# 20 of 22 gate/up pairs of a feed-forward input layer by seven half-size products (Strassen's scheme)

## The chip, the cores and the metric

The kernel runs on one core of one Trainium2 chip. The metric is the device time of one execution in microseconds; the median of three executions of the kernel before is 1820.36 us. Engines are named as in the profile: PE (TensorE matmul), PEld (TensorE weight load), DVE (VectorE), ACT (ScalarE), POOL (GpSimd), SP (SyncE, which issues most DMAs).

## The reference, cut to what matters

The model is two blocks on 512 tokens of width 1024, all in float32. The change is in the feed-forward part of the first block, with D_FF = 2816 = 22 x 128:

```python
hn = rms_norm(h, g_ffn_pre[i])
f_gate, f_up = jnp.split(hn @ w_ffn_in[i], 2, axis=-1)
f = (jax.nn.silu(f_gate) * f_up) @ w_ffn_out[i]
h = h + rms_norm(f, g_ffn_post[i])

h = h + jax.nn.sigmoid(h @ w_ple_gate[i]) * (p[i] @ w_ple[i])
```

where `rms_norm(x, g)` divides each token by the root of its mean square (plus EPS = 1e-6) and multiplies by g.

## The kernel before, in words

Activations are kept transposed: a tile is 128 features by 512 tokens. A linear layer makes one 128-feature output block after another; for each it runs over the 128-feature blocks k of its input, with the weight block as the stationary operand and the tokens as the 512 moving columns, and adds up in one bank of PSUM. Every operand of a product is split into a high part (a rounded copy, made by ScalarE) and a low part (the remainder, made by VectorE), and `mm3` multiplies high by high, high by low and low by high, so that each k-block costs three matmuls.

`prep` loads one weight chunk (128 x 1024, that is eight k-blocks of one output block) into `raw` (two buffers) by a DMA on SP's queue and splits it into `whi` and `wlo` (four buffers each). `step` records work, with or without a weight chunk, in a list; `emit` walks the list and prepares chunks up to two steps ahead of use. That is the order in the source. The order in which instructions stand on each engine is set afterwards by the framework's planner, so an engine's queue can differ from the order of the source. `auxps("mm")` (`mmps`) has five PSUM banks and `auxps("aux")` three. `tmp` is a set of four scratch tiles, `sgt` one of three.

Around the change the work runs thus. `w_out` closes the branch part; its last four output blocks are done by `linear_halves`, first for tokens 0 to 255, then for 256 to 511 with the weights held, and after each half `to_ffn` normalises, adds to `h`, makes the split input `S["B"]` of the feed-forward layer (not yet divided by the root mean square) and that divisor's inverse as a row, `S["R"]`. Then come eight small products (`ple`), written out to DRAM for later. The input layer `w_ffn_in` takes its 44 output blocks in the order gate 0, up 0, gate 1, up 1, ...; pair 0 goes by `linear_halves`, the rest by `linear`, 512 columns wide. `f_in` takes a finished block out of PSUM: a gate block is multiplied by R, passed through SiLU and multiplied by R again; an up block is multiplied by that and split at once into the pair `S["f"][j]`, which the output layer `w_ffn_out` reads. That layer has 22 input blocks, in chunks of 8, 8 and 6, and its last two output blocks are again done in halves. `to_ple` then normalises the result with `rstd_tm` and `rowcast` (small matmuls that sum squares over features and spread the result, and a chain of short VectorE steps), adds to `h`, and feeds `w_ple_gate`, which reloads the eight `ple` tiles.

The helpers hold most line numbers of the profile: L113 is a ScalarE copy (`acopy`), L116 a VectorE operation of two tensors (`tt`), L125 one with a scalar too (`stt`), L168 to L170 are the three matmuls of `mm3`, L205 and L216 the small matmuls of `rstd_tm` and `rowcast`, L697 the SiLU.

Of the kernel before, what the change touches and what calls it, by code (L numbers as in the profile page):

```python
# [15 lines left out]
P = 128  # L16
# [27 lines left out]
def build(tc, d, out):  # L44
# [17 lines left out]
    def fill(pool, taken):  # L62

        n = -taken % LINE
        if n:
            pool.tile([P, n // 4], F32, name="fill")

    fill(tiny, 46 * 32)

# [15 lines left out]
    def blk(pool, tag, bufs, dt=F32, shape=(P, T)):  # L85
        return pool.tile(list(shape), dt, tag=tag, bufs=bufs, name=tag)

    def tmp():
        return blk(small, "t", 4)
# [57 lines left out]
            return self.tiles[i][:, c.start - i * T:c.stop - i * T]  # L147

    def prep(src, hold=None):
        n = src.shape[-1]  # L150
        raw = wp.tile([P, D], F32, tag="raw", bufs=2, name="raw")
        nc.sync.dma_start(raw[:, :n], src)
        if hold is not None:
            hi, lo = [], []
            for c0 in range(0, n, T):
                h, l = hold(), hold()
                m = min(n - c0, T)
                split(raw[:, c0:c0 + m], h[:, :m], l[:, :m])
# [8 lines left out]
    def mm3(ps, wh, wl, xh, xl, first, last):
        pe.matmul(ps, wh, xh, start=first, stop=False)  # L168
        pe.matmul(ps, wh, xl, start=False, stop=False)  # L169
        pe.matmul(ps, wl, xh, start=False, stop=last)  # L170

    def bcast_mid(ap2, n):
        return ap2.unsqueeze(1).to_broadcast([ap2.shape[0], n, ap2.shape[1]])
# [22 lines left out]
        stt(out, t, 5.0, y, ALU.add, ALU.mult)  # L196
        return out

    def rstd_tm(sqs, scale, c=ALL, out=None, tag=""):

        b0, b1 = c.start // P, c.stop // P
        ps = auxps()
        for b in range(b0, b1):
            for i, s in enumerate(sqs):
                pe.matmul(ps[:, b - b0:b - b0 + 1], s[:, (b - b0) * P:(b - b0 + 1) * P], ones[:, 0:1],  # L205
                          start=(i == 0), stop=(i == len(sqs) - 1))
        m = tiny.tile([P, b1 - b0], F32, tag="rs_m" + tag, bufs=2, name="rs_m")
        ts(m, ps[:, :b1 - b0], scale, EPS, ALU.mult, ALU.add)
        return rsqrt_small(m, [P, b1 - b0], out, tag)

    def rowcast(y):

# [76 lines left out]

                step(fn, d[name][n][:, k0 * P:k1 * P], bg)  # L290

    def linear_halves(name, nbs, kb, xs, consume, then=None, hold=None):

        held = {}
        for hf, c in enumerate(HALVES):
            order = [(n, k) for n in nbs for k in kchunks(kb)]
            if hf:
                order.sort(key=lambda nk: nk[1])
            for n, (k0, k1) in order:
                def body(n=n, k0=k0, k1=k1, c=c):  # L300
# [303 lines left out]
    def load_h():  # L604
        st1.close()
        S["hp"] = hp.enter_context(tc.tile_pool(name="hp", bufs=1, reuse_waits="tile"))
        S["pf"] = st2.enter_context(tc.tile_pool(name="pf", bufs=1, reuse_waits="tile"))
        for n in range(NB):
            S["h"][n] = blk(S["hp"], "h", 8)
            nc.scalar.dma_start(S["h"][n], d["xT"][n])  # L610
        S["p"] = []
        for k in range(2):
            t = tmp()
            nc.scalar.dma_start(t, d["pT"][k])
            hi, lo = blk(S["pf"], "fh", 14, F32R), blk(S["pf"], "fh", 14, F32R)
# [13 lines left out]
            S["ss"].add(ps, c)  # L629
        return fn  # L630

    w_out_post = post("g_mix_post", lambda: blk(S["pf"], "fh", 14))

    def to_ffn(c):

        r = rowcast(rstd_tm(S["ss"].parts(c), 1.0 / D, c))
        if c.start == 0:
            S["B"] = [pair("B") for _ in range(NB)]
            S["R"] = blk(small, "R", 1)
            S["ss2"] = SqSum(lambda c: blk(S["pf"], "sx", 2, shape=(P, T // 2)))  # L640
# [13 lines left out]
        acopy(S["R"][:, c], rowcast(rstd_tm(S["ss2"].parts(c), 1.0 / D, c)))  # L654
# [5 lines left out]
    linear_halves("w_out", range(4, NB), 8, xa, w_out_post, to_ffn,  # L660
                  hold=lambda n, k0: (lambda: blk(S["pf"], "fl", 14, F32R)) if n >= 5 else None)

    S["pd"] = [None] * NB

# [21 lines left out]
        return pair(set_)  # L686


    def f_in(n, ps, c):
        R = S["R"][:, c]  # L690
        j = n % NF
        if n < NF:
            if j not in S["sigs"]:
                S["sigs"][j] = sgt()
            t = S["sigs"][j][:, c]
            tt(t, ps, R, ALU.mult)
            act.activation(out=t, in_=t, func=AF.Silu)  # L697
# [12 lines left out]
    ffn_post = post("g_ffn_post", lambda: blk(acts, "th", 8))  # L710


    S["xd"] = [None] * NB

    def to_ple(c):
        r = rowcast(rstd_tm(S["ss"].parts(c), 1.0 / D, c))
# [10 lines left out]
        return (lambda: blk(acts, "tl", 8, F32R)) if n == NB - 1 and k0 < 16 else None  # L727

    linear("w_ffn_out", range(NB - 2), NF, lambda k: S["f"][k], ffn_post)
    linear_halves("w_ffn_out", [NB - 2, NB - 1], NF, lambda k: S["f"][k], ffn_post, to_ple, hold_ffn)  # L730

    def ple_gate(n, ps, c):
        if n == 0 and c.start == 0:
            S["B"] = [None] * NB
            S["pw"] = {}
            S["ss"] = SqSum()
            S["ss"].acc = blk(small, "sq", 3)
        if n not in S["pw"]:
            S["pw"][n] = blk(S["pf"], "fh", 14)
# [649 lines left out]
```

## Time and profile before

| | |
|---|---|
| median of 3 executions | 1820.36 us (1819.8 to 1820.97) |
| profiled execution | 1820.43 us, of which its span 1818.7 us |
| granted TensorE clock | 0.997 |
| busy in the span | PE 1802.5, PEld 1485.9, DVE 1171.5, ACT 743.3 us |
| bytes moved | 189.57 MB, 104 GB/s |
| loads of `w_ffn_in` | 44 of 512 KB, 3.4 us each to landing |

The span runs from the first to the last instruction. Busy time counts an engine's instructions; a matmul overlaps its neighbours, so PE's busy time tells that it had work and not that it ran at its peak. In rows in order of time the first number is the start, the second the length, both in us, and brackets hold the idle time before it and what ended that. `mm<-th,whi` is a matmul that writes a tile `mm` and reads `th` and `whi`; `th` and `tl` hold the high and low parts of the input layer's activations, `fh`, `fl`, `xh`, `xl` those of f. On this time axis pair 0 begins at about 571 us, pair 1 at 583, and the output layer at about 812.

### The profile page before, as it was taken

How to read it: one execution, taken by the hardware profiler on the slowest of the kernel's cores; microseconds unless marked ns; L12 is line 12 of the kernel's file. 1: busy time of each engine (PE TensorE's matmuls, PEld its weight loads, DVE VectorE, ACT ScalarE, POOL GpSimd, SP SyncE). 2: the span in 40 equal slices, each digit the busy share in tenths (PEclk: the TensorE clock that was granted, in tenths of full speed). 3: DMA queues.
4: the chain of work that ended last, by engine and by line, in shares of the span. 5: the costliest groups of instructions: out<-in, count | busy, mean ns of one | idle time of the engine just before them, and what ended most of it. 6: DMA issues, size and time to landing. Idle time of an engine off the chain costs nothing.

```text
span 1818.7 us, 23549 instructions
## 1 busy us (share of the span) xinstructions
PE 1802.5 (99%) x9252; PEld 1485.9 (82%) x9252; DVE 1171.5 (64%) x2062; ACT 743.3 (41%) x1219; POOL 0.7 (0%) x5
## 2 busy tenths in 40 slices
PE   9999999999999999999999999999999999999997
PEld 7888888888888888888898777876678888888887
DVE  6999977996448544442367684587646577777333
ACT  5342234326346323222245762574435354444221
POOL 0000000000000000000000000000000000000000
PEclk9999999999999999999999999999999999999999
DMA  5332323332353232233335222222236322323331
GB/s 193 105 105 94 103 68 107 114 98 67 122 179 100 98 104 93 95 96 96 110 103 189 71 65 77 81 83 82 99 122 204 115 93 93 104 93 92 94 97 65
DMA packets 62895, 189.57 MB, mean 104 GB/s; under 512 B 7232, under 2 KB 10432, under 8 KB 62784
## 3 DMA queue, kind: packets, MB, share of 16 engines
q1 hardware_dynamic: 56736, 177.53, 30.2%
q10 hardware_dynamic: 6048, 10.53, 1.8%
q8 instruction: 72, 1.18, 0.3%
q14 instruction: 39, 0.32, 0.1%
HBM read 176.51 MB, written 11.53 MB: 103 GB/s over the span
## 4 chain that ended last, share of the span: by engine, by line
PE 96%; DVE 2%; ACT 1%; issue 0%; DMA 0%; SPq 0%; DVEq 0%; ACTq 0%
PE mm L169 28%; PE mm L168 28%; PE mm L170 27%; PE g L983 1%; PE att L1111 1%; PE att L170 1%; PE att L169 1%; PE att L168 1%; PE mm L340 1%; PE mm L339 1%; PE mm L341 1%; PE att L1103 1%; PE aux L216 1%; DVE wlo L116 0%; PE att L1082 0%
## 5 line engine op out<-in xcount | busy, mean ns | idle before, releaser
L113 ACT ACTIVATE whi<-raw 128x1024 fp32r<-128x1024 f32 (+3 forms) x304 | 312.3, 1027 | 658.1 <-PE mm L169 405.5
L116 DVE TENSOR_TENSOR wlo<-raw,whi 128x1024 fp32r<-128x1024 f32 (+3 forms) x304 | 359.3, 1182 | 201.2 <-ACT whi L113 198.8
L168 PE MATMUL mm<-xh,whi 128*128 128x512 f32 (+1 forms) x1032 | 393.7, 382 | 0.0
L169 PE MATMUL mm<-xl,whi 128*128 128x512 f32 (+1 forms) x1032 | 393.2, 381 | 0.0
L170 PE MATMUL mm<-xh,wlo 128*128 128x512 f32 (+1 forms) x1032 | 393.1, 381 | 0.0
L169 PE MATMUL mm<-tl,whi 128*128 128x512 f32 (+1 forms) x976 | 379.9, 389 | 0.1
L168 PE MATMUL mm<-th,whi 128*128 128x512 f32 (+1 forms) x976 | 380.0, 389 | 0.0
L170 PE MATMUL mm<-th,wlo 128*128 128x512 f32 (+1 forms) x976 | 378.1, 387 | 0.0
L170 PEld LDWEIGHTS mm<-xh,wlo 128*128 128x128 f32 x1032 | 194.0, 188 | 37.3
L168 PEld LDWEIGHTS mm<-xh,whi 128*128 128x128 f32 x1032 | 193.9, 188 | 37.0 <-issue 0.2
L169 PEld LDWEIGHTS mm<-xl,whi 128*128 128x128 f32 x1032 | 194.0, 188 | 36.7 <-issue 0.2
L168 PEld LDWEIGHTS mm<-th,whi 128*128 128x128 f32 x976 | 183.5, 188 | 38.8 <-issue 4.3
L169 PEld LDWEIGHTS mm<-tl,whi 128*128 128x128 f32 x976 | 183.7, 188 | 36.6 <-issue 2.1
L170 PEld LDWEIGHTS mm<-th,wlo 128*128 128x128 f32 x976 | 183.6, 188 | 35.6 <-issue 1.0
L125 DVE SCALAR_TENSOR_TENSOR cv<-hc,vec,cv 128x507 f32<-128x507 f32 (+18 forms) x240 | 173.0, 736 | 4.2 <-ACT cv L462 0.6
L170 PE MATMUL mm<-fh,wlo 128*128 128x512 f32 (+1 forms) x252 | 91.0, 361 | 0.0
L168 PE MATMUL mm<-fh,whi 128*128 128x512 f32 (+1 forms) x252 | 90.8, 360 | 0.0
L116 DVE TENSOR_TENSOR sg<-mm,R 128x512 f32<-128x512 f32 (+1 forms) x43 | 29.1, 678 | 95.8 <-PE mm L170 95.7
L169 PE MATMUL mm<-fl,whi 128*128 128x512 f32 (+1 forms) x236 | 84.6, 358 | 0.0
L116 DVE TENSOR_TENSOR t<-mm,R 128x512 f32<-128x512 f32 x56 | 38.5, 688 | 54.0 <-PE mm L170 52.0
L116 DVE TENSOR_TENSOR t<-mm,sg 128x512 f32<-128x512 f32 (+1 forms) x31 | 20.9, 674 | 62.5 <-PE mm L170 62.5
L170 PEld LDWEIGHTS mm<-fh,wlo 128*128 128x128 f32 x252 | 47.6, 189 | 7.1
(385 smaller groups left out, 1998.7 us busy)
## 6 DMA issues: line engine op xcount, KB each, us to landing
raw<-in_w_ffn_in SPq DMA_DIRECT2D x44, 512.0 KB, 3.4
raw<-in_w_up SPq DMA_DIRECT2D x44, 512.0 KB, 3.4
raw<-in_w_g SPq DMA_DIRECT2D x24, 512.0 KB, 3.4
raw<-in_w_out SPq DMA_DIRECT2D x16, 512.0 KB, 3.5
raw<-in_w_ffn_out SPq DMA_DIRECT2D x16, 512.0 KB, 3.5
raw<-in_w_gab SPq DMA_DIRECT2D x16, 512.0 KB, 3.4
raw<-in_w_down SPq DMA_DIRECT2D x16, 512.0 KB, 3.6
raw<-in_w_qkv SPq DMA_DIRECT2D x12, 512.0 KB, 3.6
```

The costliest lines, as they stand in the source:

```text
L113: act.activation(out=o, in_=i, func=AF.Copy, scale=scale)
L116: dve.tensor_tensor(out=o, in0=a, in1=b, op=op)
L125: dve.scalar_tensor_tensor(out=o, in0=a, scalar=s, in1=b, op0=op0, op1=op1)
L168: pe.matmul(ps, wh, xh, start=first, stop=False)
L169: pe.matmul(ps, wh, xl, start=False, stop=False)
L170: pe.matmul(ps, wl, xh, start=False, stop=last)
L216: pe.matmul(r[:, b * P:(b + 1) * P], y[:, b:b + 1].to_broadcast([P, P]), ident, start=True, stop=True)
L339: pe.matmul(ps, xh[:, t], wh[:, c], start=(k == 0), stop=False)
L340: pe.matmul(ps, xh[:, t], wl[:, c], start=False, stop=False)
L341: pe.matmul(ps, xl[:, t], wh[:, c], start=False, stop=(k == kb - 1))
L983: pe.matmul(c3(out)[e, b], w(e, b), c3(m)[e, b], start=True, stop=True)
L1103: pe.transpose(pt[:, c:c + P], z[:, c:c + P], ident)
```

## The change

Pairs 0 and 1 stay as they are. For each of pairs 2 to 21 the weights are seen as a 2 x 2 array of blocks a11, a12 (gate, input blocks 0 to 3 and 4 to 7) and a21, a22 (up, the same), and the input as b11, b12 (input blocks 0 to 3, tokens 0 to 255 and 256 to 511) and b21, b22 (blocks 4 to 7). Eight block products become seven, each over four k-blocks, 256 tokens wide and still by `mm3`; the combined weights are formed for every pair on VectorE, the combined activations once (`wino_x`). Products 1, 6, 7, 4 add up in one bank, 5 and 3 in another, 2 has one of its own; partial results are copied or added out between them. A pair's weight groups are {1, 2}, {6, 5}, {7, 3} and {4}; product 4 is done after product 1 of the next pair.

f is written raw by the pairs and split for all 22 blocks in one step (`f_split`) ahead of the output layer. The factor R on f is left out, and the norm behind the output layer makes up for it (`rstd_tm` with `by`, from the kept `S["Rf"]`). The output layer's second half goes through its chunks and k-blocks in reverse. Several buffers have other tags.

```diff
-    def rstd_tm(sqs, scale, c=ALL, out=None, tag=""):
+    def rstd_tm(sqs, scale, c=ALL, out=None, tag="", by=None):
...
+        stt(m, ps[:, :b1 - b0], scale, by, ALU.mult, ALU.mult)
+        tt(m, m, by, ALU.mult)
+        ts(m, m, EPS, None, ALU.add)
+        y = rsqrt_small(m, [P, b1 - b0], out, tag)
+        tt(y, y, by, ALU.mult)
+        return y
...
+    def f_raw(j):
+        S["f"][j] = (blk(S["pf"], "fr", 6) if j < 6 else blk(acts, "xh", 8) if j < 14
+                     else blk(acts, "xl", 8) if j < 21 else tmp())
...
             tt(t, ps, S["R"][:, c], ALU.mult)
             act.activation(out=t, in_=t, func=AF.Silu)
-            tt(t, t, R, ALU.mult)
         else:
-            t = tmp()[:, c]
-            tt(t, ps, S["sigs"][j][:, c], ALU.mult)
-            ...
-            split(t, hi[:, c], lo[:, c])
+            tt(S["f"][j][:, c], ps, S["sigs"][j][:, c], ALU.mult)
...
+    def wino_x(k):
+        x = []
+        for i in (k, 4 + k):
+            x.append(tmp())
+            acopy(x[-1], S["h"][i], v("g_ffn_pre", i))
+        b1, b2 = x
+        r12, r34 = tmp(), tmp()
+        tt(r12[:, H0], b1[:, H1], b1[:, H0], ALU.subtract)
+        tt(r12[:, H1], b2[:, H1], r12[:, H0], ALU.subtract)
+        tt(r34[:, H0], b2[:, H1], b1[:, H1], ALU.subtract)
+        tt(r34[:, H1], b2[:, H0], r12[:, H1], ALU.subtract)
+        for i, r in ((1, r12), (3, r34)):
+            hi, lo = blk(S["pf"], "tc", 16, F32R), blk(S["pf"], "tc", 16, F32R)
+            split(r, hi, lo)
...
+    XOP = {1: 11, 2: 21, 3: 22, 4: 4, 5: 1, 6: 2, 7: 3}
+    FEW = {0: (1, 2), 1: (6, 5), 2: (7, 3), 3: (4,)}
...
+    def weights(p, g):
+        if g == 0:
+            r0 = wp.tile([P, D], F32, tag="raw", bufs=2, name="raw")
+            r1 = blk(S["pf"], "wr", 2, F32, (P, D))
+            nc.sync.dma_start(r0, d["w_ffn_in"][p])
+            nc.sync.dma_start(r1, d["w_ffn_in"][NF + p])
...
+        if g == 1:
+            src = w["c"] = blk(S["pf"], "ws", 1, F32, (P, D))
+            tt(a11, a11, a21, ALU.subtract)
+            tt(src[:, L], a22, a11, ALU.subtract)
+            tt(src[:, R], a21, a22, ALU.add)
+        elif g == 2:
+            tt(a12, a12, w["c"][:, L], ALU.subtract)
+        elif g == 3:
+            src = a22
...
+        split(src, hi[:, :n], lo[:, :n])
+        return hi, lo
...
+    def product(p, m, wh, wl):
+        w = ws.setdefault(p, {})
+        if m in (1, 5, 2):
+            w[m] = (auxps() if m == 2 else mmps())[:, H0]
+        y = w[{1: 1, 6: 1, 7: 1, 4: 1, 5: 5, 3: 5, 2: 2}[m]]
+        for k in range(4):
+            b = slice(k * P, (k + 1) * P)
+            xh, xl = ET[XOP[m], k]
+            mm3(y, wh[:, b], wl[:, b], xh, xl, k == 0 and m in (1, 5, 2), k == 3, skip_group_check=True)
+        if m == 1:
+            w["t"], w["v"], w["sg"] = tmp(), tmp(), sgt()
+            acopy(w["t"][:, H0], y)
+        elif m == 2:
+            tt(w["sg"][:, H0], y, w["t"][:, H0], ALU.add)
+        elif m == 6:
+            acopy(w["t"][:, H1], y)
+        elif m == 5:
+            acopy(w["v"][:, H0], y)
+        elif m == 7:
+            w["f"] = f_raw(p)
+            tt(w["f"][:, H1], y, w["v"][:, H0], ALU.add)
+        elif m == 3:
+            sg = w["sg"]
+            tt(sg[:, H1], y, w["t"][:, H1], ALU.add)
+            tt(sg, sg, S["R"], ALU.mult)
+            act.activation(out=sg, in_=sg, func=AF.Silu)
+            tt(w["f"][:, H1], w["f"][:, H1], sg[:, H1], ALU.mult)
+        else:
+            tt(w["f"][:, H0], y, w["sg"][:, H0], ALU.mult)
 
     order = [n for j in range(NF) for n in (j, NF + j)]
     linear_halves("w_ffn_in", order[:2], 8, xb, f_in)
-    linear("w_ffn_in", order[2:], 8, xb, f_in)
+    for k in range(2):
+        step(lambda k=k: wino_x(k))
+    linear("w_ffn_in", order[2:3], 8, xb, f_in)
+    for k in range(2, 4):
+        step(lambda k=k: wino_x(k))
+    linear("w_ffn_in", order[3:4], 8, xb, f_in)
...
+        if due is None:
+            products(p, 0, (1, 2))
+        else:
+            products(p, 0, (1,))
+            products(due, 3, (4,), [(p, 0, 2)])
+        products(p, 1, (6, 5))
+        products(p, 2, (7, 3))
+        due = p
+    if due is not None:
+        products(due, 3, (4,))
+
+    def f_split():
...
+        for j in range(NF):
+            raw = S["f"][j]
+            S["f"][j] = hi, lo = new(j), new(j)
+            split(raw, hi, lo)
+
+    step(f_split)
...
-        r = rowcast(rstd_tm(S["ss"].parts(c), 1.0 / D, c))
+        r = rowcast(rstd_tm(S["ss"].parts(c), 1.0 / D, c, by=S["Rf"][:, c.start // P:c.stop // P]))
...
-    linear_halves("w_ffn_out", [NB - 2, NB - 1], NF, lambda k: S["f"][k], ffn_post, to_ple, hold_ffn)
+    linear_halves("w_ffn_out", [NB - 2, NB - 1], NF, lambda k: S["f"][k], ffn_post, to_ple, hold_ffn, back=True)
```

The combined activations go to 16 tiles of a buffer set `tc`; `f_split` writes blocks 0 to 7 into these same tiles, 8 to 10 into the raw weight buffers `wr` and `ws`, and the rest into `fr`, `xh` and `xl`, which held raw f.

More of the change, by code (lines that the diff above doesn't have):

```diff
@@ L66, in fill @@
             pool.tile([P, n // 4], F32, name="fill")
-    fill(tiny, 46 * 32)
+    fill(tiny, 47 * 32)
     def lined(n):
@@ L149, in prep @@
     def prep(src, hold=None):
+        if callable(src):
+            return src()
         n = src.shape[-1]
@@ L165, in prep, with mm3 @@
         return hi, lo
[L167 to L170, printed above, removed]
+    def mm3(ps, wh, wl, xh, xl, first, last, **kw):
+        pe.matmul(ps, wh, xh, start=first, stop=False, **kw)
+        pe.matmul(ps, wh, xl, start=False, stop=False, **kw)
+        pe.matmul(ps, wl, xh, start=False, stop=last, **kw)
     def bcast_mid(ap2, n):
@@ L207, in rstd_tm @@
         m = tiny.tile([P, b1 - b0], F32, tag="rs_m" + tag, bufs=2, name="rs_m")
-        ts(m, ps[:, :b1 - b0], scale, EPS, ALU.mult, ALU.add)
-        return rsqrt_small(m, [P, b1 - b0], out, tag)
+        if by is None:
+            ts(m, ps[:, :b1 - b0], scale, EPS, ALU.mult, ALU.add)
+            return rsqrt_small(m, [P, b1 - b0], out, tag)
+        stt(m, ps[:, :b1 - b0], scale, by, ALU.mult, ALU.mult)
[4 more added lines that the diff above has]
+        return y
     def rowcast(y):
@@ L290, in linear, with linear_halves @@
                 step(fn, d[name][n][:, k0 * P:k1 * P], bg)
-    def linear_halves(name, nbs, kb, xs, consume, then=None, hold=None):
+    def linear_halves(name, nbs, kb, xs, consume, then=None, hold=None, back=False):
         held = {}
@@ L297, in linear_halves, with body @@
             if hf:
-                order.sort(key=lambda nk: nk[1])
+                order.sort(key=lambda nk: nk[1], reverse=back)
             for n, (k0, k1) in order:
-                def body(n=n, k0=k0, k1=k1, c=c):
-                    if k0 == 0:
+                ks = list(range(k0, k1))
+                first, last = 0, kb - 1
+                if hf and back:
+                    ks.reverse()
+                    first, last = last, first
+                def body(n=n, k0=k0, ks=ks, first=first, last=last, c=c):
+                    if first in ks:
                         held[n, "ps"] = mmps()
@@ L304, in body @@
                     wh, wl = held[n, k0]
-                    for k in range(k0, k1):
+                    for k in ks:
                         xh, xl = xs(k)
                         w = slice((k - k0) * P, (k - k0 + 1) * P)
-                        mm3(ps, wh[:, w], wl[:, w], xh[:, c], xl[:, c], k == 0, k == kb - 1)
-                    if k1 == kb:
+                        mm3(ps, wh[:, w], wl[:, w], xh[:, c], xl[:, c], k == first, k == last)
+                    if last in ks:
                         consume(n, ps, c)
@@ L614, in load_h @@
             nc.scalar.dma_start(t, d["pT"][k])
-            hi, lo = blk(S["pf"], "fh", 14, F32R), blk(S["pf"], "fh", 14, F32R)
+            hi, lo = blk(S["pf"], "fr", 6, F32R), blk(S["pf"], "fr", 6, F32R)
             split(t, hi, lo)
@@ L630, in post @@
         return fn
-    w_out_post = post("g_mix_post", lambda: blk(S["pf"], "fh", 14))
+    w_out_post = post("g_mix_post", lambda: blk(S["pf"], "tc", 16))
     def to_ffn(c):
@@ L653, in to_ffn @@
                 S["ss2"].add(h, c)
-        acopy(S["R"][:, c], rowcast(rstd_tm(S["ss2"].parts(c), 1.0 / D, c)))
+        if c.start == 0:
+            S["Rf"] = tiny.tile([P, NT], F32, tag="Rf", bufs=1, name="Rf")
+        r = S["Rf"][:, c.start // P:c.stop // P]
+        rstd_tm(S["ss2"].parts(c), 1.0 / D, c, out=r)
+        acopy(S["R"][:, c], rowcast(r))
         if c.start:
@@ L659, in build, with two, new, hold_out @@
     linear("w_out", range(4), 8, xa, w_out_post)
-    linear_halves("w_out", range(4, NB), 8, xa, w_out_post, to_ffn,
-                  hold=lambda n, k0: (lambda: blk(S["pf"], "fl", 14, F32R)) if n >= 5 else None)
+    def two(tag, bufs):
+        kept = []
+        def new():
+            if not kept:
+                t = blk(S["pf"], tag, bufs, F32R, (P, D))
+                kept.extend((t[:, :T], t[:, T:]))
+            return kept.pop(0)
+        return new
+    def hold_out(n, k0):
+        if n < 5:
+            return None
+        return two("wr", 2) if n == 7 else (lambda: blk(S["pf"], "tc", 16, F32R))
+    linear_halves("w_out", range(4, NB), 8, xa, w_out_post, to_ffn, hold=hold_out)
     S["pd"] = [None] * NB
@@ L686, in f_pair @@
         return pair(set_)
+    def f_raw(j):
+        S["f"][j] = (blk(S["pf"], "fr", 6) if j < 6 else blk(acts, "xh", 8) if j < 14
+                     else blk(acts, "xl", 8) if j < 21 else tmp())
+        return S["f"][j]
     def f_in(n, ps, c):
[L690 removed]
         j = n % NF
@@ L695, in f_in @@
             t = S["sigs"][j][:, c]
-            tt(t, ps, R, ALU.mult)
+            tt(t, ps, S["R"][:, c], ALU.mult)
             act.activation(out=t, in_=t, func=AF.Silu)
-            tt(t, t, R, ALU.mult)
         else:
-            t = tmp()[:, c]
-            tt(t, ps, S["sigs"][j][:, c], ALU.mult)
             if S["f"][j] is None:
-                S["f"][j] = f_pair(j, "A")
-            hi, lo = S["f"][j]
-            split(t, hi[:, c], lo[:, c])
+                f_raw(j)
+            tt(S["f"][j][:, c], ps, S["sigs"][j][:, c], ALU.mult)
@@ new lines, in build @@
+    H0, H1 = HALVES
+    ET = {}
+    def wino_x(k):
[12 more added lines that the diff above has]
+            split(r, hi, lo)
+            for e, c in enumerate(HALVES):
+                ET[i + e, k] = hi[:, c], lo[:, c]
+        for i, (n, c) in ((11, (k, H0)), (21, (4 + k, H0)), (22, (4 + k, H1))):
+            ET[i, k] = tuple(t[:, c] for t in xb(n))
@@ new lines, in build @@
+    XOP = {1: 11, 2: 21, 3: 22, 4: 4, 5: 1, 6: 2, 7: 3}
+    L, R = slice(0, T), slice(T, D)
+    FEW = {0: (1, 2), 1: (6, 5), 2: (7, 3), 3: (4,)}
+    wr = {}
+    def weights(p, g):
[4 more added lines that the diff above has]
+            nc.sync.dma_start(r1, d["w_ffn_in"][NF + p])
+            wr[p] = dict(a=r0, b=r1)
+        w = wr[p]
+        a11, a12, a21, a22 = (w[x][:, c] for x in "ab" for c in (L, R))
+        src = w["a"]
+        if g == 1:
[7 more added lines that the diff above has]
+            src = a22
+        n = src.shape[-1]
+        hi = wp.tile([P, D], F32R, tag="whi", bufs=4, name="whi")
+        lo = wp.tile([P, D], F32R, tag="wlo", bufs=4, name="wlo")
+        split(src, hi[:, :n], lo[:, :n])
+        return hi, lo
@@ new lines, in build @@
+    ws = {}
+    def product(p, m, wh, wl):
[27 more added lines that the diff above has]
+            tt(w["f"][:, H0], y, w["sg"][:, H0], ALU.mult)
@@ L707, in build, with products, fn @@
     order = [n for j in range(NF) for n in (j, NF + j)]
     linear_halves("w_ffn_in", order[:2], 8, xb, f_in)
-    linear("w_ffn_in", order[2:], 8, xb, f_in)
+    for k in range(2):
[4 more added lines that the diff above has]
+    linear("w_ffn_in", order[3:4], 8, xb, f_in)
+    kept = {}
+    def products(p, g, ms, after=()):
+        def fn(wh, wl):
+            kept[p, g] = wh, wl
+            for q, g2, m in [(p, g, m) for m in ms] + list(after):
+                c = (L, R)[FEW[g2].index(m)]
+                wh, wl = kept[q, g2]
+                product(q, m, wh[:, c], wl[:, c])
+        step(fn, lambda: weights(p, g))
@@ new lines, in build @@
+    PLAIN = ()
+    due = None
+    for p in range(2, NF):
+        if p in PLAIN:
+            linear("w_ffn_in", [p], 8, xb, f_in)
+            if due is not None:
+                products(due, 3, (4,))
+            due = None
+            linear("w_ffn_in", [NF + p], 8, xb, f_in)
+            continue
+        if due is None:
[6 more added lines that the diff above has]
+        due = p
@@ new lines, in build, with new @@
+    if due is not None:
+        products(due, 3, (4,))
+    def f_split():
+        wide, wide2 = two("wr", 2), two("ws", 1)
+        def new(j):
+            if 8 <= j < 10:
+                return wide()
+            if j == 10:
+                return wide2()
+            if j < 14:
+                return blk(S["pf"], *(("tc", 16) if j < 8 else ("fr", 6)), F32R)
+            return blk(acts, "xh" if j < 18 else "xl", 8, F32R)
+        for j in range(NF):
+            raw = S["f"][j]
+            S["f"][j] = hi, lo = new(j), new(j)
+            split(raw, hi, lo)
@@ L738, in ple_gate @@
         if n not in S["pw"]:
-            S["pw"][n] = blk(S["pf"], "fh", 14)
+            S["pw"][n] = blk(S["pf"], "tc", 16)
             nc.sync.dma_start(S["pw"][n], S["pd"][n])
```

## The prediction

> **What bounds the kernel now.** I read the page first, then busy time by stretch, then single instructions in order of time, then the waits.
>
> ```profile
> span 1818.7 us, 23549 instructions
> ...
> PE 1802.5 (99%) x9252; PEld 1485.9 (82%) x9252; DVE 1171.5 (64%) x2062; ACT 743.3 (41%) x1219; POOL 0.7 (0%) x5
> ...
> DVE  6999977996448544442367684587646577777333
> ...
> PEclk9999999999999999999999999999999999999999
> ...
> PE 96%; DVE 2%; ACT 1%; issue 0%; DMA 0%; SPq 0%; DVEq 0%; ACTq 0%
> ```
>
> TensorE is busy and the chain that ended last runs 96% through it, at full clock. A change gains here only by giving TensorE less to stream, and loses wherever another engine then keeps it waiting. Columns of the next view: the stretch, its length, then busy time and count of PE, PEld, DVE, ACT.
>
> ```profile
> 60.00:180.00 120.00, 120.00 (x564) 100.52 (x563) 118.22 (x177) 43.26 (x52) 0.00 (x0) 1.00 0.29 97
> 594.00:812.00 218.00, 218.00 (x964) 180.56 (x963) 100.52 (x120) 63.12 (x80) 0.00 (x0) 1.00 0.30 96
> 571.50:594.00 22.50, 22.50 (x150) 20.57 (x149) 21.34 (x56) 14.28 (x28) 0.00 (x0) 1.00 0.34 112
> ```
>
> The 20 pairs of the change are the second row: 218 us of nothing but 512-column matmuls, VectorE at 46%. The first row shows that VectorE at 98.5% need not hold TensorE up. The third, the way into the pairs, is already 95% VectorE.
>
> **Price of a half-width matmul.** The change trades 512-column matmuls for more of 256 columns. Pair 0 already runs in halves, so the trace has both. In order of time (start, length):
>
> ```profile
> 571.57 0.28 PE L168 MATMUL mm<-th,whi 128*128 128x256 f32 x1
> ...
> 582.97 0.28 PE L170 MATMUL mm<-th,wlo 128*128 128x256 f32 x1
> 583.09 0.40 PE L168 MATMUL mm<-th,whi 128*128 128x512 f32 x1
> ...
> 573.01 0.19 PEld L169 LDWEIGHTS mm<-tl,whi 128*128 128x128 f32 x1
> 573.13 0.19 PEld L170 LDWEIGHTS mm<-th,wlo 128*128 128x128 f32 x1
> ```
>
> From 571.57 to 583.09 lie pair 0's 96 half-width matmuls (two outputs, two halves, 8 k-blocks, 3 passes): 11.52/96 = 0.120 us each. In the 218 us row there are 964 at full width, about two of them cut at the edges: 218/962 = 0.2266. Half width costs 53% of full width, not half. A pair before is 2 outputs x 8 k-blocks x 3 passes = 48 x 0.2266 = 10.88 us; after, 7 products x 4 k-blocks x 3 passes = 84 x 0.120 = 10.08. Gain 0.80 us a pair, 16.0 in 20.
>
> The Trainium skill, "TensorE: Matmul & The Clock Gate", Back-to-back issue gap, gives 518 cycles for 512 columns and 262 for 256; at its 2.4 GHz 48 x 215.8 ns less 84 x 109.2 ns would be 1.19 us a pair, 23.7 in all (an estimate from that page). The rows decide against it: a fixed 13 ns stands on each matmul here. The same page, in Part 3, says that a weight load overlaps running matmuls only for another row group; that would count against 84 loads instead of 48, but the loads above start 0.12 us apart though each lasts 0.19, so by that rule too the trace disagrees.
>
> **Price of the added VectorE and ScalarE work.** What counts is start to start when an engine is packed:
>
> ```profile
> 439.91 4.27 DVE L116 TENSOR_TENSOR cv<-cv,aux 128x512 f32<-128x512 f32 x7
> ...
> 554.12 0.42 DVE L116 TENSOR_TENSOR h<-h,fh 128x256 f32<-128x256 f32 x1
> 554.45 0.48 DVE L125 SCALAR_TENSOR_TENSOR tl<-h,vec,th 128x256 fp32r<-128x256 f32 x1
> ...
> 600.65 0.69 DVE L116 TENSOR_TENSOR sg<-mm,R 128x512 f32<-128x512 f32 x1 [2.75 <-PE mm L170]
> 601.51 1.23 DVE L116 TENSOR_TENSOR wlo<-raw,whi 128x1024 fp32r<-128x1024 f32 x1 [0.18 <-ACT whi L113]
> 602.66 0.68 DVE L116 TENSOR_TENSOR sg<-sg,R 128x512 f32<-128x512 f32 x1
> ...
> 600.42 1.06 ACT L113 ACTIVATE whi<-raw 128x1024 fp32r<-128x1024 f32 x1 [3.86 <-PE mm L169]
> 601.39 0.62 ACT L697 ACTIVATE sg<-sg 128x512 f32<-128x512 f32 x1
> ...
> 445.69 4.27 ACT L113 ACTIVATE th<-cv 128x512 fp32r<-128x512 f32 x8
> ...
> 542.27 0.47 ACT L113 ACTIVATE fh<-mm,vec 128x256 f32<-128x256 f32 x1 [0.76 <-PE mm L170]
> 542.64 0.38 ACT L227 ACTIVATE sq<-mm 128x256 f32<-128x256 f32 x1
> ```
>
> VectorE: 512 columns (4.27 - 0.69)/6 = 0.60, 256 columns 0.33, 1024 columns 1.14 (601.51 to 602.66, rounded down as the follower was ready). ScalarE: 0.97 for 1024, 0.53 for 512, 0.37 for 256 from PSUM. Three rows also show that queues are not in source order: the low part of a later weight block stands between the two halves of one eviction, so a planner fills idle engine time.
>
> Per pair, VectorE after: four half-block weight sums 4 x 0.60 = 2.40; low parts of three full and one half block 3 x 1.14 + 0.60 = 4.02; evictions of products 2, 7, 3, 4 and the final gate product 5 x 0.33, scaling by R 0.60: 2.25. Sum 8.67, under TensorE's 10.08 by 1.41 us (before: 2 x 1.14 + 4 x 0.60 = 4.68 of 10.88). ScalarE: 3 x 0.97 + 0.53 + 3 x 0.37 + 0.53 = 5.1. TensorE stays the bound of a pair if the planner spends VectorE's slack well. Weight buffers give room: product 1's block is free again after product 2 and due two steps later, 5.8 us, for a ScalarE copy and a subtraction of 2.3.
>
> The tight place is ScalarE's copy of product 6 (then of 5): product 7 (then 3) accumulates into the same bank, one product (12 x 0.12 = 1.44 us) later. Copy 0.38 plus the 0.28 tail of the last matmul fit with 0.8 left, but not behind a 1024-column copy begun just before (0.97). Bounds: 0 to 0.2 us each, 0 to 8 us over 40 copies. I take 0.8, near the low end, because the planner's timing has been near the chip's: the view of waits gives
>
> ```profile
> PE aux L216 <- DVE rs_y L125: 2.9, 5, 2.2
> ```
>
> that is, of the small matmuls it places behind VectorE's chains, one waited 2.2 us and the other four 0.7 together.
>
> **The way in.** Sums of the activations (four blocks of input, each 4 half-width VectorE steps, two 512-column splits, two scaled copies) must precede product 6 of pair 2. VectorE: 4 x (4 x 0.33 + 2 x 0.60) = 10.1 us, plus three weight sums 1.8. VectorE is packed from here on:
>
> ```profile
> 571.54 0.75 DVE L116 TENSOR_TENSOR fh<-fh,aux 128x256 f32<-128x256 f32 x2 [0.87 <-PE aux L216]
> ...
> 593.55 0.42 DVE L116 TENSOR_TENSOR xl<-t,xh 128x256 fp32r<-128x256 f32 x1
> 595.21 0.69 DVE L116 TENSOR_TENSOR t<-mm,sg 128x512 f32<-128x512 f32 x1 [1.24 <-PE mm L170]
> ...
> 586.46 0.34 PE aux L205 x4
> 590.09 0.53 PE aux L216 x4
> ```
>
> It runs out of work at 594.0. Taken out before that: three scalings by R (2 x 0.33 + 0.60), two splits of f (0.66), and one weight block not yet due (1.14): 3.1. So product 6 is ready at 594.0 - 3.1 + 10.1 + 1.8 = 602.8. TensorE would be there at 583.09 + 48 x 0.2266 + 0.87 for the row sums among them (the last two rows) + 24 x 0.120 = 597.7. Stall 5.1; bounds 0 (the planner defers evictions and square sums) to 10 (the chain of copies, sums, copy, subtraction through four scratch buffers runs with holes). I take 5.
>
> **The way out.** f is no longer split pair by pair but in one step of 22 splits ahead of the output layer: VectorE 22 x 0.60 = 13.2, ScalarE 22 x 0.53 = 11.7.
>
> ```profile
> 808.07 0.96 DVE L116 TENSOR_TENSOR wlo<-raw,whi 128x768 fp32r<-128x768 f32 x1
> ...
> 812.61 0.39 PE L168 MATMUL mm<-xh,whi 128*128 128x512 f32 x1
> ```
>
> TensorE consumes an f block every 3 x 0.2266 = 0.68 us, slower than 0.60, so it can follow; but the third weight block of the first output, which before was ready 4 us ahead of that layer (808.07 against 812.61), now stands behind the splits and is due after 16 x 0.68 = 10.9 us. Splits 13.2, last eviction 0.33 and this block 0.9 make 14.4: 3.5 us late without a head start, none if VectorE, which has no next pair to prepare in the last 10 us, does six splits early. Only the destinations free up late (four of them 4.3 us before the end). I take 1.5, bounds 0 to 4.
>
> **Small parts.** Leaving R out of f makes the norm behind the output layer three small VectorE steps longer,
>
> ```profile
> 940.35 0.16 DVE L116 TENSOR_TENSOR rs_t<-rs_m,rs_y 128x2 f32<-128x2 f32 x1
> 940.54 0.16 DVE L125 SCALAR_TENSOR_TENSOR rs_t<-rs_t,rs_y 128x2 f32<-128x2 f32 x1
> ```
>
> 0.2 us each, 0.6 in a chain that feeds the next layer closely: 0.5 (bounds 0 and 1.2, both halves). Weight bytes and SP's issues are the same two 512 KB blocks a pair; SP issues both at a pair's first step, waits at most for the buffer of two pairs earlier, and nothing due sooner queues behind. The reversed order of the output layer's second half frees the first f buffers last, and these take the eight reloads on SP that were issued at 929.0 to 933.5 before; they now start at about 932 and are needed from 941: nothing, up to 2 us if late. Other renamed buffers: nothing, since each is free when asked for.
>
> **Sum**, against the profiled execution's 1820.43 us (0.07 over the median of 1820.36): -16.0 + 0.8 + 5 + 1.5 + 0.5 = -8.2, so 1812.
>
> **Rivals.**
> *In and out hidden.* The planner starts activation sums and splits early enough. For it: ScalarE is 63% busy in the stretch before 594; against it: VectorE's 95%. Time 1820.4 - 16.0 + 1 = 1805.
>
> *Transitions dearer.* The way in costs 10 and the way out 4, or the copies 8: 1818 to 1822, no difference.
>
> *VectorE's queue binds every pair (slower).* Two of the four weight blocks are summed on VectorE, copied on ScalarE (1.06) and subtracted on VectorE. If the order leaves VectorE idle across both copies, a pair is 8.67 + 2 x 1.15 = 11.0 us, longer than 10.88: 1820.4 + 2 + 7.8 = 1830. It decides from about 1.8 us of uncovered idling a pair (8.67 + 1.8 = 10.47: 0.41 gained x 20 = 8.2, all spent on the ends). For it: a pair now passes eleven times between ScalarE and VectorE, the old one six times (weight block twice, gate twice, split twice). Against it: the first stretch above, VectorE 98.5% busy and TensorE unbroken, though its filler work depended on no matmul. The Trainium skill, "VectorE: DVE Perf Modes", The DRAIN you can't avoid, has the next VectorE step start only once the pipe is empty. That would make lengths, not starts, add up; the rows here overlap by 0.08 us (601.51 + 1.23 against 602.66).
>
> **Chances.** Forecast (1808 to 1817) 0.46; hidden 0.12; dearer 0.18; slower (1824 to 1838) 0.24. Two runs of this kernel are told apart from about 0.2%, 3.6 us: faster 0.46 + 0.11 = 0.57, same 0.19, slower 0.24. The range 1804 to 1831 takes in the first three and half of the last; the likeliest case's own is 1808 to 1817.
>
> **What would show it.** Right: 84 half-width matmuls a pair, 0.120 apart, a pair every 10.1 us; VectorE about 86% in the pairs; one TensorE gap near 597 to 603 waiting for VectorE; a smaller one 11 us into the output layer, behind a weight block. Wrong: a pair over 10.4 us with TensorE waiting for weight blocks or for ScalarE's copies; half-width spacing above 0.125; no gap at 597.

## The result, and the profile after

Median of the changed kernel 1809.13 us (1808.77 to 1812.59, four runs), of the kernel before in the same set 1820.08 (1819.25 to 1820.97); ratio 0.9942, interval 0.9929 to 0.9954. So 0.58% faster, 2.9 us under the forecast of 1812. The profiled execution took 1808.77 us (span 1807.0) against 1820.43 (1818.7).

The page of the kernel after:

```profile
span 1807.0 us, 25347 instructions
PE 1787.1 (99%) x9972; PEld 1506.2 (83%) x9972; DVE 1271.6 (70%) x2268; ACT 807.4 (45%) x1334; POOL 0.7 (0%) x5
...
DVE  6999977996448999992286784586546577777333
...
PE 92%; DVE 4%; ACT 2%; DMA 1%; issue 1%; SPq 0%; DVEq 0%; ACTq 0%
```

TensorE has 720 more matmuls and 15 us less to do; 20 x (84 - 48) = 720, so the whole difference in count is the change. VectorE's digits for the slices of the pairs, 5 and 4 before, are 9. The chain of waits still runs through TensorE, but 4% of it is now VectorE. Busy time by stretch of the kernel after (length; busy time and count of PE, PEld, DVE, ACT, POOL; clock, DMA share, GB/s):

```profile
594.00:604.00 10.00, 6.92 (x53) 6.28 (x53) 10.00 (x21) 7.85 (x16) 0.00 (x0) 1.00 0.00 1
604.00:799.40 195.40, 195.40 (x1630) 195.40 (x1630) 180.38 (x280) 110.48 (x167) 0.00 (x0) 1.00 0.34 105
799.40:811.40 12.00, 11.26 (x47) 7.92 (x46) 11.66 (x19) 7.45 (x13) 0.00 (x0) 1.00 0.28 86
```

Way in, pairs, way out. In the first row VectorE is busy for all of 10 us while TensorE lacks three. In the second TensorE never pauses: 195.4/1630 = 0.120 us a matmul, with VectorE at 92%. One pair, from the first matmul of one of its products to the same one of the next pair, in order of time:

```profile
610.78 0.28 PE L170 MATMUL mm<-tc,whi 128*128 128x256 f32 x1
...
620.86 0.28 PE L170 MATMUL mm<-tc,whi 128*128 128x256 f32 x1
```

10.08 us, as forecast. The way in, TensorE (the bracket gives the idle time before, and what ended it):

```profile
597.49 0.28 PE L170 MATMUL mm<-tc,whi 128*128 128x256 f32 x1
598.12 0.38 PE L171 MATMUL mm<-tc,whi 128*128 128x256 f32 x1 [0.35 <-DVE tc L116]
598.35 0.28 PE L172 MATMUL mm<-tc,wlo 128*128 128x256 f32 x1
600.47 0.38 PE L170 MATMUL mm<-tc,whi 128*128 128x256 f32 x1 [1.84 <-ACT t L113]
...
602.33 0.28 PE L172 MATMUL mm<-tc,wlo 128*128 128x256 f32 x1
603.49 0.39 PE L170 MATMUL mm<-th,whi 128*128 128x256 f32 x1 [0.88 <-ACT whi L113]
```

Start to start beyond 0.120 us: 0.51 before 598.12, 2.00 before 600.47, 1.04 before 603.49, and smaller ones; 4.0 together. The largest is put down to ScalarE's copy of a product; ScalarE's and VectorE's own rows say who was late:

```profile
600.03 0.38 ACT L113 ACTIVATE t<-mm 128x256 f32<-128x256 f32 x1 [1.29 <-DVE t L116]
```

```profile
599.18 1.09 DVE L116 TENSOR_TENSOR t<-t 128x256 f32<-128x256 f32 x3
```

ScalarE, next in its queue, stood 1.29 us idle for a VectorE step on a scratch buffer, one of the three sums of activations in the second row. The last of the three gaps is put down to a copy of weights that stood behind this one in ScalarE's queue. The way out, TensorE and then VectorE:

```profile
803.58 0.45 PE L170 MATMUL mm<-tc,whi 128*128 128x512 f32 x1
804.30 0.50 PE L171 MATMUL mm<-tc,whi 128*128 128x512 f32 x1 [0.28 <-DVE tc L116]
...
804.88 0.40 PE L170 MATMUL mm<-tc,whi 128*128 128x512 f32 x1
805.50 0.50 PE L171 MATMUL mm<-tc,whi 128*128 128x512 f32 x1 [0.23 <-DVE tc L116]
```

```profile
803.55 0.69 DVE L116 TENSOR_TENSOR tc<-fr,tc 128x512 fp32r<-128x512 f32 x1
804.15 0.69 DVE L116 TENSOR_TENSOR xl<-xl 128x512 fp32r<-128x512 f32 x1
804.76 0.69 DVE L116 TENSOR_TENSOR tc<-xh,tc 128x512 fp32r<-128x512 f32 x1
...
807.17 0.96 DVE L116 TENSOR_TENSOR wlo<-raw,whi 128x768 fp32r<-128x768 f32 x1
```

Each f block of these has a start 0.72 or 0.62 us after the one before it instead of 0.23: its low part came late. VectorE makes one low part in `tc` in 1.2 us here, because a split of another set (`xl`, `xh`, `fr`) stands between each two.

Where the span's 11.7 us come from: 20 pairs of 10.08 instead of 10.88 (218/962 x 48) -16.0; way in +4.0; way out +2.0; TensorE's first weights, long before the change and different in every execution, -1.0; about -0.7 not assigned.

### The profile page after: what moved, and what is told of

Read it like the earlier page. It is cut to its first block, busy times and chain, and to the rows that moved or that the text cites. A ratio compares the mean times of both kernels' runs of the same rounds, so it can differ in the third digit from the quotient of the medians.

```text
span 1807.0 us, 25347 instructions
## 1 busy us (share of the span) xinstructions
PE 1787.1 (99%) x9972; PEld 1506.2 (83%) x9972; DVE 1271.6 (70%) x2268; ACT 807.4 (45%) x1334; POOL 0.7 (0%) x5
## 3 DMA queue, kind: packets, MB, share of 16 engines
q1 hardware_dynamic: 56736, 177.53, 31.1%
## 4 chain that ended last, share of the span: by engine, by line
PE 92%; DVE 4%; ACT 2%; DMA 1%; issue 1%; SPq 0%; DVEq 0%; ACTq 0%
PE mm L171 26%; PE mm L170 26%; PE mm L172 26%; PE g L1165 1%; DVE wlo L116 1%; ACT whi L113 1%; PE att L1293 1%; PE att L172 1%; PE att L171 1%; PE att L170 1%; PE mm L355 1%; PE mm L356 1%; PE att L1285 1%; PE mm L354 1%; DMA raw<-in_w_sv 1%
## 5 line engine op out<-in xcount | busy, mean ns | idle before, releaser
L170 PE MATMUL mm<-th,whi 128*128 128x512 f32 (+1 forms) x816 | 300.2, 369 | 0.9 <-ACT whi L113 0.9
L171 PE MATMUL mm<-tl,whi 128*128 128x512 f32 (+1 forms) x816 | 300.3, 368 | 0.1
L172 PE MATMUL mm<-th,wlo 128*128 128x512 f32 (+1 forms) x816 | 298.6, 366 | 0.0
L170 PEld LDWEIGHTS mm<-th,whi 128*128 128x128 f32 x816 | 153.9, 189 | 27.5 <-issue 4.3
L171 PEld LDWEIGHTS mm<-tl,whi 128*128 128x128 f32 x816 | 154.2, 189 | 24.4 <-issue 2.1
L172 PEld LDWEIGHTS mm<-th,wlo 128*128 128x128 f32 x816 | 154.1, 189 | 23.0 <-issue 1.0
L170 PE MATMUL mm<-tc,whi 128*128 128x256 f32 (+1 forms) x384 | 113.8, 297 | 1.8 <-ACT t L113 1.8
L171 PE MATMUL mm<-tc,whi 128*128 128x256 f32 (+1 forms) x384 | 114.4, 298 | 1.1 <-DVE tc L116 1.1
L172 PE MATMUL mm<-tc,wlo 128*128 128x256 f32 (+1 forms) x384 | 113.7, 296 | 0.0
L171 PEld LDWEIGHTS mm<-tc,whi 128*128 128x128 f32 x384 | 73.5, 191 | 4.5 <-DVE tc L116 2.8
L170 PEld LDWEIGHTS mm<-tc,whi 128*128 128x128 f32 x384 | 73.4, 191 | 4.3 <-ACT t L113 2.0
L172 PEld LDWEIGHTS mm<-tc,wlo 128*128 128x128 f32 x384 | 73.5, 191 | 1.7
```

The source lines that it names most:

```text
L170: pe.matmul(ps, wh, xh, start=first, stop=False, **kw)
L171: pe.matmul(ps, wh, xl, start=False, stop=False, **kw)
L172: pe.matmul(ps, wl, xh, start=False, stop=last, **kw)
```

## The experiments

The theory: all the gain is TensorE's, 0.80 us a pair; VectorE's steps add by their starts, so that it has 1.41 us to spare in a pair; the way in is VectorE's backlog of sums; the way out is a matter of which tiles come free when. The rivals: VectorE's lengths add (it would have almost nothing to spare), scratch buffers make the way in, or the third weight block the way out. The way-in and way-out stalls below are TensorE's start-to-start times beyond 0.120 and 0.2267 us.

**All pairs plain.** The scheme taken back, the split of f at the output layer and the rest kept:

```
-    for k in range(2):
-        step(lambda k=k: wino_x(k))
...
-    PLAIN = ()
+    PLAIN = tuple(range(2, NF))
```

> All 22 pairs plain, everything else of the change kept (f raw, split in one step, R left out, reversed second half). Theory: the gain is the matmuls' alone; without them stand the old 1820.1 and what the way out costs, 0 to 2 us (VectorE has more time here, so the splits can start early): 1820 to 1822. Rival: part of the gain comes from the lighter evictions and the moved splits: 1815 to 1819.

Measured 1820.29, ratio 0.9999 (0.9989 to 1.0008). What else the change moves costs nothing and gains nothing while VectorE has room.

**An eighth product.** In `product`, each pair runs product 2 twice (its result is changed by that):

```
-        for k in range(4):
+        for k in list(range(4)) * (2 if m == 2 else 1):
```

> Product 2 is streamed twice into its bank (the second time from the start), so a pair has 8 products. Theory: TensorE bounds the pairs, so each grows by 12 x 0.120 = 1.44 us: 20 x 1.44 = 28.8, less up to 2 us of the stall on the way in: 1836 to 1838, which is slower than before by 20 x (96 x 0.120 - 48 x 0.2266) = 12.9 and the ends. Rival: VectorE or ScalarE bounds the pairs, so part of the added time is hidden: below 1830.

Measured 1840.2, ratio 1.0108 (1.0094 to 1.0122), 31.1 over the changed kernel. One product more turns the gain into a loss. Busy time in the pairs, and the place of the rest, in order of time:

```profile
620.00:780.00 160.00, 160.00 (x1316) 158.40 (x1315) 127.02 (x194) 73.74 (x110) 0.00 (x0) 1.00 0.30 91
```

```profile
696.84 1.06 ACT L113 ACTIVATE whi<-ws 128x1024 fp32r<-128x1024 f32 x1 [0.99 <-PE mm L171]
697.80 0.37 ACT L113 ACTIVATE t<-mm 128x256 f32<-128x256 f32 x1
698.03 0.28 PE L172 MATMUL mm<-tc,wlo 128*128 128x256 f32 x1
698.22 0.39 PE L170 MATMUL mm<-th,whi 128*128 128x256 f32 x1
698.45 0.28 PE L171 MATMUL mm<-tl,whi 128*128 128x256 f32 x1
```

160 us hold 1316 matmuls, 96 a pair: 11.67 us a pair where 96 x 0.120 = 11.52. The remainder is where the prediction put its bound of 0 to 0.2: a copy out of PSUM (697.80) stands behind a 1024-column copy of weights, the next product of that bank starts at 698.22 when it is done, and the two starts there are 0.19 and 0.23 apart instead of 0.12: 0.18 us. Twenty such remainders, some 3 us, are why the time came out above its forecast. In the changed kernel itself it is zero.

**VectorE's room.** Two and four repeats of the last low part of each pair, 512 columns, 0.60 us each by starts:

```
+        if g == 3:
+            for _ in range(2):        # 4 in the second kernel
+                tt(lo[:, :n], src, hi[:, :n].bitcast(F32), ALU.subtract)
```

> The low part of the half block of each pair is formed three times instead of once: two more VectorE steps of 512 columns. Theory (starts add up, 8.67 us of VectorE a pair): 8.67 + 2 x 0.60 = 9.87, still under 10.08, so the pairs stay 10.08 us apart: 1809 to 1810. Rival (lengths add up; VectorE's busy share of the pairs was 91.8%, 9.26 us): 9.26 + 2 x 0.69 = 10.64, so 0.56 us more a pair: about 1820.

> Formed five times: four more steps. Theory: 8.67 + 4 x 0.60 = 11.07 us, VectorE is now the bound and a pair takes that: 0.99 x 20 = 20, about 1829. Rival (lengths add up): 9.26 + 4 x 0.69 = 12.0, 1.94 x 20 = 39, about 1848.

Two: 1816.09, ratio 0.9978 (0.9968 to 0.9988). Four: 1835.31, ratio 1.0083 (1.0068 to 1.0098). Busy time in the pairs, two first, then four:

```profile
620.00:780.00 160.00, 160.00 (x1323) 158.89 (x1322) 156.67 (x252) 80.35 (x127) 0.00 (x0) 1.00 0.31 103
```

```profile
620.00:780.00 160.00, 152.75 (x1218) 147.46 (x1217) 158.99 (x260) 74.04 (x113) 0.00 (x0) 1.00 0.28 93
```

With two, 1323 matmuls in 160 us make 10.16 us a pair: VectorE has 9.87 by starts and just fits; by lengths 10.6 was due. With four, a pair takes 11.09 us from start to start, against 8.67 + 2.40 = 11.07 by starts and 12.0 by lengths. Starts it is: the 92% busy in the changed kernel is 86% of the pair's time by starts, and the rest overlap. The forecast rival "VectorE's queue binds every pair" is a real cliff, but 1.4 us a pair away. Two repeats were to cost nothing and cost 7 us, of which the pairs have 20 x 0.08 = 1.6. The rest lies at the ends (way in 6.9 instead of 4.0, way out 4.6 instead of 2.0), and of these 5.5 us about 4 are no wait for VectorE: up to 601.5 the gaps on the way in are those of the changed kernel, and then TensorE's clock fell (last section). The kernel with four repeats lies 6 us above its forecast of 1829, about 4 of them from the clock too.

**The way in.** Four kernels. One pair more of plain form between the first pairs and the scheme (19 pairs by it, about 10 us more for the sums):

```
-    PLAIN = ()
+    PLAIN = (2,)
```

> Pair 2 is done plainly too, 19 pairs by products. Theory: the 4.0 us in which TensorE stood on its way into the first product pair come from VectorE being packed there; 10.9 us more of plain matmuls ahead of it let VectorE catch up, so the stall goes and one pair's 0.80 us of gain goes with it: 1809.1 - 3.9 + 0.8 = about 1806. Rival: the stall belongs to the start of the product pairs as such (the scratch tiles and the order in which the planner places the first products), so it only moves by one pair: 1809.1 + 0.8 = about 1810, with a gap of some 4 us ten us later.

Measured 1808.62, ratio 0.9933 (0.992 to 0.9945). Way in, then way out:

```profile
594.00:604.00 10.00, 10.00 (x47) 8.33 (x47) 9.86 (x24) 6.99 (x14) 0.00 (x0) 1.00 0.05 21
799.00:811.00 12.00, 10.14 (x40) 6.79 (x39) 11.10 (x18) 6.54 (x11) 0.00 (x0) 1.00 0.23 80
```

The way-in stall is gone, but the time missed its 1806 by 2.6 and can't be told from that of the changed kernel: the way out grew from 2.0 to 3.4, and in this profile the program's start cost 1.5 more. Five scratch tiles instead of four:

```
-        return blk(small, "t", 4)
+        return blk(small, "t", 5)
```

> Five scratch tiles instead of four, nothing else. Theory: the stall on the way into the pairs is VectorE's backlog, which a tile doesn't shorten: the gaps stay at 3 to 4 us, 1808.5 to 1809.5. Rival: the copy of product 1 stood behind VectorE only because its scratch tile was held by an activation sum; with one more tile the 2.1 us gap goes: about 1807.

Measured 1811.09, ratio 0.9951 (0.9935 to 0.9968). The gaps still come to 4.2 us, only in other places, and something new follows:

```profile
594.00:604.00 10.00, 7.40 (x54) 6.42 (x53) 10.00 (x23) 7.31 (x13) 0.00 (x0) 1.00 0.00 0
604.40:607.40 3.00, 2.92 (x13) 2.92 (x14) 2.17 (x3) 0.82 (x3) 0.00 (x0) 0.50 0.47 143
```

One more buffer doesn't help: VectorE stays busy for all of 10 us. The time came out above both forecasts, by about what the clock in the second row cost (last section). The 16 half-width subtractions left out, so that the plain scaled activations go into the products (the output is another):

```
-        r12, r34 = tmp(), tmp()
-        tt(r12[:, H0], b1[:, H1], b1[:, H0], ALU.subtract)
-        ...
+        r12, r34 = b1, b2
```

> The four half-width subtractions per input block that form the combined activations are left out (the blocks are split as they are), so the output isn't the reference's. That takes 16 x 0.33 = 5.3 us from VectorE and two scratch tiles per block. Theory: the backlog on the way in (4.0 us of TensorE gaps) is gone: about 1805.2. Rival: the gaps are set by the order on ScalarE (scaled copies, splits and the copy of product 1 in one queue), which is unchanged: 1808 to 1809.

Measured 1806.28, ratio 0.9922 (0.9909 to 0.9936):

```profile
594.00:604.00 10.00, 9.53 (x79) 9.25 (x78) 9.81 (x19) 5.65 (x10) 0.00 (x0) 1.00 0.33 104
```

Stall 0.8 instead of 4.0: 5.3 us less for VectorE took 3.2 us off TensorE. The edit also takes two scratch tiles fewer for each pair of input blocks; but the plain pair, which leaves the tiles as they are and only gives VectorE time, took the stall away too, and a fifth tile did not. So it is the backlog. The same subtractions moved to GpSimd, with the destinations of the next part:

```
+    def gg(o, a, b, op):
+        nc.gpsimd.tensor_tensor(out=o, in0=a, in1=b, op=op)
...
-        tt(r12[:, H0], b1[:, H1], b1[:, H0], ALU.subtract)
+        gg(r12[:, H0], b1[:, H1], b1[:, H0], ALU.subtract)
```

> The same sixteen subtractions on GpSimd, which is idle here, with all 20 pairs by products and the split's other destinations (1807.4 by themselves). No row shows GpSimd's time for such a step. Theory: if a step takes under about 1 us there, VectorE's backlog goes and nothing else is given up: 1807.4 - 4.0 = about 1803.5. Rival: GpSimd is slower than that, or slows VectorE down beside it, and TensorE waits for GpSimd on its way in: 1808 or more.

Measured 1812.23, ratio 0.9959 (0.9945 to 0.9972): slower than leaving them on VectorE. Groups by line, then VectorE in order of time:

```profile
L748 POOL TENSOR_TENSOR t<-t 128x256 f32<-128x256 f32 x16 | 14.6, 926 | 551.9 <-ACT t L113 547.5 <-ACT sx L236 2.8 <-DVE tc L116 0.6
```

```profile
592.72 0.70 DVE L122 TENSOR_SCALAR rs_y<-rs_i 128x2 int32<-128x2 int32 x1
593.94 0.69 DVE L116 TENSOR_TENSOR rs_t<-rs_m,rs_y 128x2 f32<-128x2 f32 x1
602.10 0.15 DVE L125 SCALAR_TENSOR_TENSOR Rf<-rs_t,rs_y 128x2 f32<-128x2 f32 x1
```

A subtraction takes 0.93 us on GpSimd, and beside it VectorE's two-column steps take 0.70 instead of 0.15. The norm's chain, made of such steps, reached its last one at 602.1 (at 593.6 in the changed kernel), and TensorE waited for it:

```profile
PE aux L225 <- DVE Rf L125: 4.8, 1, 4.8
```

**The way out.** Blocks 4, 5 and 6 of f go to the raw weight buffers, which are free early, and blocks 8 to 10 to `tc` instead:

```
-            if 8 <= j < 10:
+            if 4 <= j < 6:
...
-            if j == 10:
+            if j == 6:
...
-                return blk(S["pf"], *(("tc", 16) if j < 8 else ("fr", 6)), F32R)
+                return blk(S["pf"], *(("tc", 16) if j < 11 else ("fr", 6)), F32R)
```

> In the step that splits f, blocks 4 to 6 take the weight buffers that come free early and blocks 8 to 10 take the tiles of the combined activations that come free late. Theory: the 1.8 us that TensorE stood at f blocks 4 to 7 on its way into the output layer come from the late tiles; only block 7 is still late, so some 1.3 us are gained: about 1807.8. Rival: VectorE's and ScalarE's throughput sets it, whatever the tiles: no change, 1809.1, and the same 1.8 us of gaps.

Measured 1807.42, ratio 0.9928 (0.9915 to 0.994); the intervals of this kernel and of the changed one overlap, the trace does not leave it open:

```profile
799.00:811.00 12.00, 12.00 (x58) 9.90 (x57) 12.00 (x21) 8.35 (x15) 0.00 (x0) 1.00 0.16 46
```

TensorE is busy throughout; stall 0.1 instead of 2.0, though the third weight block is ready later than before, at 809.7 instead of 808.1. So the choice of tiles was the cause, not that block. That the `tc` tiles delay these splits by coming free last is inferred: the last product's matmul that reads `tc` starts at 799.3, just ahead of the layer's first at 799.4.

**Both ends mended.** The plain pair and these destinations together:

> Pair 2 plain and the other destinations of the split step together. Theory: both stalls are gone, the one on the way in (4.0 us, bought with 0.8 us of one pair's gain) and the one on the way out (1.8 us, which grew to 3.3 us when pair 2 alone was made plain): 1809.1 - 4.0 + 0.8 - 1.8 = about 1804.1, and the stretch of the pairs without a gap. Rival: a stall taken away at one end comes back as work left over at the other, as it did with pair 2 alone: 1806 to 1808.

Measured 1804.44, ratio 0.9913 (0.9899 to 0.9928), the best version found. Way in, pairs, way out:

```profile
594.00:604.00 10.00, 10.00 (x47) 8.33 (x46) 9.86 (x24) 5.91 (x12) 0.00 (x0) 1.00 0.00 1
604.00:790.00 186.00, 186.00 (x1546) 185.76 (x1545) 168.94 (x260) 102.92 (x154) 0.00 (x0) 1.00 0.31 101
796.00:811.00 15.00, 15.00 (x73) 12.60 (x72) 13.31 (x23) 9.16 (x16) 0.00 (x0) 1.00 0.29 79
```

No idle time is left in any of the three: 19 x 0.80 = 15.2 us off 1820 is 1805, the time that the prediction gave to "in and out hidden".

**The change itself again**, run beside the kernel without the sums and the one with the sums on GpSimd:

> The changed kernel itself, for its times on the chip of these runs and a second look at its way in. Theory: 1808.5 to 1809.5, with 4.0 us of gaps between 597 and 604. If TensorE's clock falls after those gaps in this execution, as it did with five scratch tiles, up to 3 us more.

Measured 1809.81 (1809.46 to 1810.03), ratio 0.9942 (0.9929 to 0.9954); way in 4.0, way out 2.0, as in the first profile.

## Why the prediction was right

- *Price of a half-width matmul, 0.120 us, and 10.08 a pair:* right to the digit; 16.0 of gain in the pairs, and the kernel without the scheme shows that there is no other.
- *VectorE 8.67 a pair, under TensorE by 1.41:* right, by starts. The two kernels with repeats put the edge between 1.2 us, which still nearly fitted, and 2.4 us. By busy time the forecast 86% reads 92%, since lengths overlap; the row alone would have misled.
- *ScalarE's copies +0.8:* oversized, 0 in this kernel. The mechanism exists: it appears at 0.15 to 0.18 us a pair when the eighth product shifts the order.
- *Way in +5:* 4.0, at the place forecast (597 to 604) and by VectorE's backlog, as shown by the plain pair and by the sums left out; not as one wait for the sums, though: half of it went through a copy on ScalarE that waited for one.
- *Way out +1.5:* size right (2.0) by luck, step wrong. The prediction had the third weight block late, 11 us into the layer. That block was ready at 808.1, 4 us ahead of its need, and TensorE waited 3 to 8 us into the layer for f blocks whose `tc` tiles come free last. The prediction had that as a side remark ("Only the destinations free up late"); it was the whole, as the other destinations showed.
- *Norm +0.5:* TensorE's wait behind its chains is 0.3 us in all, 0.4 before: 0. *Reloads, renamed buffers:* nothing, as forecast.

By the prediction's own terms -16.0 + 0 + 4.0 + 2.0 + 0 = -10.0 instead of -8.2; the unrelated start and the unassigned part make up the rest of the profiled 11.7. Of the rivals, "hidden" took two small edits more, and "VectorE binds" needed more than two more VectorE steps a pair; "transitions dearer" came nearest with two of them (way in 6.9, way out 4.6), and there by the clock.

## What to carry to other kernels

What a scheme of fewer but narrower products saves is worked out from the trace's own matmul spacings: here half width costs 0.53 of full, and an eighth off the arithmetic became 7% off the pairs. Check the next engine by start-to-start times, not busy share. Then look at both transitions: the set-up work needs a stretch in which its engine has room (one plain pair more), and the first tiles needed afterwards must go into buffers that come free first; here that was worth 4.7 us more, beside the 11 that the change brought.

## What the runs showed of the hardware that was not expected

**The clock fell after short gaps.** In the kernel with two repeats, busy time after its way in, and TensorE in order of time:

```profile
600.00:605.00 5.00, 2.94 (x17) 2.61 (x18) 5.00 (x11) 3.96 (x8) 0.00 (x0) 0.81 0.00 0
605.00:610.00 5.00, 5.00 (x26) 5.00 (x25) 3.53 (x6) 0.50 (x1) 0.00 (x0) 0.50 0.34 105
610.00:615.00 5.00, 4.82 (x40) 4.62 (x39) 4.90 (x10) 3.30 (x5) 0.00 (x0) 1.00 0.34 108
```

```profile
609.35 0.41 PE L171 MATMUL mm<-tl,whi 128*128 128x256 f32 x1
609.56 0.41 PE L172 MATMUL mm<-th,wlo 128*128 128x256 f32 x1
609.78 0.37 PE L170 MATMUL mm<-th,whi 128*128 128x256 f32 x1
```

The granted clock is 0.50 and half-width matmuls start 0.21 us apart instead of 0.12, for some 24 of them: 24 x 0.09 = 2.2 us on top of the gaps; on the way out of the same kernel it happened once more. It happened with two and four repeats, with five scratch tiles and, after the 4.8 us wait, with GpSimd, once much later (1008.7) with an eighth product, and in neither profile of the changed kernel (4.0 us of gaps, 2.0 the longest), though with five scratch tiles the gaps sum to about the same 4.2 us and the longest is 1.3. The Trainium skill, "TensorE: Matmul & The Clock Gate", Why this matters for your kernels, warns of TensorE gaps over about 3 us; the GpSimd kernel's 4.8 agrees, but with two repeats no single gap was longer than 2.0 and with five scratch tiles none than 1.3, so here the measurement decides: shorter gaps close together can do it.

What separates the profiles shows when their records of the granted clock are laid beside TensorE's work. In all of them the clock changes only in steps of 3.41 us, counted from a start that differs by execution. One such step each on the way in, of the changed kernel, of two repeats and of five scratch tiles:

```profile
599.39:602.81 3.42, 2.14 (x15) 1.91 (x15) 3.42 (x8) 2.78 (x5) 0.00 (x0) 1.00 0.00 0
599.72:603.13 3.41, 1.65 (x13) 1.62 (x14) 3.41 (x9) 2.12 (x5) 0.00 (x0) 1.00 0.00 0
600.84:604.25 3.41, 1.86 (x12) 1.24 (x10) 3.41 (x7) 2.28 (x4) 0.00 (x0) 1.00 0.00 0
```

The first kept the clock; behind the other two it was 0.50 from the next step on, for two steps and for one. The changed kernel and two repeats have the same 2.0 us gap; in the former a step ends in its middle, in the latter nearly all of it lies in one step. Over the thirteen profiles, start and end of the program aside, eight steps at full clock were followed by a fall, and in each of them TensorE had started matmuls of at most 3328 columns together; in every other step it was at least 3328, against some 7280 for packed half-width matmuls (3.41/0.120 = 28.4 of 256 columns). So in these traces the clock fell where TensorE did less than about 45% of its packed work within one step, and where the steps lie on the gaps is chance. No run sets this count apart from other measures of the same idle time.

**GpSimd beside VectorE** is dear for small steps: 0.15 became 0.70 above, and the norm's chain paid 4.8 us of TensorE. The Trainium skill, "SBUF — State Buffer", Terms, says that the two share a port pair which one holds for a whole instruction while the other is blocked; the rows agree, a two-column step waiting out most of a 0.93 us subtraction.
